# Six small moves in a one-layer hybrid decoder kernel: a third W buffer, later output products, a shorter head norm, a later z load, the norm row by DMA, a later turn for the gates

## The chip, the cores and the metric

The kernel runs on one core of a Trainium2 chip. The metric is the device time of one execution in microseconds (us), as the median of several runs. The engines are TensorE (PE in the profile; PEld is its weight load), VectorE (DVE), ScalarE (ACT), GpSimd (POOL) and SyncE (SP). SP and POOL are used here to issue DMAs. Each engine works through its own queue in a fixed order; between engines there are only semaphores.

## The reference

One layer of a decoder trunk for 1024 prompt rows and 8 single-token samples, all in float32, width 1024. The input is normalised by RMS and a gain row, goes through one combined projection (`w_in`, 1024 x 7176), and then through two branches. Cut to what matters here:

```python
hn = rmsnorm(x, g_norm)
xa, za, uq, uk, uv, uo, zb, ui, uf = split(hn @ w_in)
yA = rglru_branch(xa, ...)                     # gated linear recurrence
hB = mlstm_seq(uq, uk / 16, uv, ui + b_mi, log_sigmoid(uf + b_mf), ...)
# per chunk of 128 rows and head:
#   w = exp(D - m_t);  P = w * (q k^T)
#   num = P v + ginter * (q C);  den = sum(P) + ginter * (q n)
#   h = num / max(|den|, exp(-m_t));  C, n carried to the next chunk
yB = sigmoid(uo) * hB
yB = yB * rsqrt(mean(yB * yB) + EPS) * g_mhead # per head
merged = concat(yA * silu(za), yB * silu(zb))
y = rmsnorm(x + merged @ w_out, g_final)
```

The states of both branches are outputs too.

## The kernel before

**Precision.** Products run on float32r operands. Each operand is split in a high and a low half (`split`, L70 and L71: ScalarE writes the high half, VectorE the low one), and `mm3` (L64 to L66) makes three matmuls of each product.

**Order.** The source is written for a tile framework which gives every instruction its place in its engine's queue before the kernel runs. So the order of the source is not always the order of a queue, and each step is best followed in the profile's lines. A tile from a pool with `bufs=n` shares n buffers with the tiles of the same tag: a load into it waits until the tile n places earlier has been read for the last time.

**Start.** Nine row tiles of x (one of them the samples) are loaded by `x_fetch`; `x_stats` takes the sum of squares on ScalarE and the reciprocal root (L180, L184 to L188); `x_turn` multiplies by the root and by `gn_b`, the gain row broadcast to 128 partitions (L381), and transposes on TensorE (L385); `x_split` splits the transposed halves out of PSUM; `plain` makes the first products, with the weights `hi`, `lo` (first 256 columns and the 8 gate columns) and `w1` (the next 256). The broadcast row is made on TensorE from a loaded row `grow` and a matrix of ones (L488) and copied out of PSUM by VectorE (L490) and ScalarE (L492). Eight dummy matmuls (`warm_up`, L472) surround it.

**Projection.** Units of 512 columns (`UNITS`) are worked off with a scheme of seven products over half-size blocks (`cb`, `Q_P1` to `Q_P7`); `prep` makes and splits the weights of each, two products ahead. After every half of a product `pop_bg` takes the next steps from three lists: `bg` (two steps in the first and the last unit, else one), `rgq` (the recurrence) and `dcq` (the samples). `gates()` is a generator on `bg`: it loads parameters, makes the gate rows, two scans (L593, L594), the stacked rows `stk` (L612 to L615), yields eight times, transposes `stk` on TensorE (L622) and writes `be_t`, `gi_t`, `de_t`, `em_t`. `rd_open`, after it on the list, opens the pool for the recurrence and the samples and starts their loads.

**The mLSTM loop.** An item is a chunk of 128 rows and one head: n = 4c + h, 32 items. `m_load(n)` loads W (the row `d_alpha`, broadcast to 128 partitions, two buffers), qk and vt on SP's queue. `m_k(n)` makes the exponent of W (L1045 on VectorE, L1046 on ScalarE) and splits q and the state. `m_a(n)` makes S and the turned k on TensorE (L1065, L1067) into the PSUM tile `s`, of which there is one, and on VectorE `pf` (L1074, the last reader of W) and `kl` (L1075). `m_b(n)` makes the products with the state, k and v and updates the state (L1126). `m_g(n)` applies the output gate and takes the sum of squares per head. At h = 0 `m_n(c-1)` makes the norm of the chunk's four heads (L1151 to L1156, then `rsqrt`); at h = 1 `m_z(c-1, pair)` transposes the heads (L1173, into the PSUM tiles `s` and `qp`), multiplies by z (L1176) and splits.

**Output.** `out_part` makes the products with `w_out`, for a row tile c and a half of the columns; it's a generator on `work`, and `fill(k)` runs k of its pieces. Every item has four of them, placed between `m_a`, `m_k` and `m_b`. When a row tile is complete, L1272 adds x, and `finish` makes the norm and multiplies both halves by it and by the final gain (L1226) and stores them from POOL's queue (L1227). The next tile's x is loaded into the same staging buffers (L1271, POOL's queue). `last_tile` has an order of its own for the last row tile.

**Entry of the loop.** After the last unit `o_load(0)`, `m_k(4)`, `z_load(0)`, `wo_load` and `wo_prep` follow: z(0) is read from `d_zs`, which the last units have written; `wo_prep` (L1212, L1213) splits the last rows of `w_out`.

**Memory.** `const` tiles live for the whole kernel; `dconst` tiles lie in a pool that is closed at `m_open2`, where the loop's second pool takes its place.

Of the kernel before, what the change touches and what calls it, by code (L numbers as in the profile page):

```python
# [17 lines left out]
P = 128  # L18
# [31 lines left out]
def hymba_kernel(  # L50
# [17 lines left out]
    def split(hi, lo, src):  # L68

        A.copy(hi, src)  # L70
        V.tensor_tensor(lo, src, hi.bitcast(F32), op=ALU.subtract)  # L71
# [7 lines left out]
    def ps(tag, shape):  # L79
        return psp.tile(shape, F32, tag=tag, name=f"ps_{tag}", bufs=NBUF.get(tag, 1))  # L80

    def const(shape, name, dt=F32):
        return cpool.tile(shape, dt, tag=name, name=name)
# [10 lines left out]
    def ws(shape, name, dt=F32R):  # L94

        return wsp.tile(shape, dt, tag="ws", name=name)
# [12 lines left out]

    idF = const([P, P], "idF")  # L110
    make_identity(nc, idF)
    ones = const([P, P], "ones")
    G.memset(ones, 1.0)
    maskT = const([P, P], "maskT")
    G.memset(maskT, 0.0)
# [247 lines left out]
    def x_fetch(i):  # L363
        xt[i] = ws([P, T], f"x{i}", F32)
        ld(xt[i][:rows_of(i)], x_prompt[0, i * P:(i + 1) * P, :] if i < 8 else x_sample[:, 0, :])
# [20 lines left out]
            xps[i].append(pt)  # L386
        del xt[i]

    def x_split(i):

        p0, p1 = xps[i]
        if i == 8:
            for half, pt in enumerate(xps[i]):
                V.tensor_copy(hnd[:, 4 * half:4 * half + 4, 0:NB], pt[:, :, 0:NB])
            return
        s = slice(i % 4 * P, (i % 4 + 1) * P)
        if i >= 4:
            b12 = [fp.tile([P, 4, P], F32R, tag=f"b12{n}", name=f"b12{n}") for n in "hl"]
            split(b12[0], b12[1], p0)
            split(cb[Q_P3][0][:, :, s], cb[Q_P3][1][:, :, s], p1)  # L400
            bf[i] = b12
        else:
            split(cb[Q_P1][0][:, :, s], cb[Q_P1][1][:, :, s], p0)
            split(cb[Q_P2][0][:, :, s], cb[Q_P2][1][:, :, s], p1)

    def x_copy(i):

# [59 lines left out]

    pw = ps("tr", [P, P])

    def warm_up(n):  # L470
        for _ in range(n):
            TE.matmul(pw, ones, ones, start=True, stop=True)  # L472
    grow = ws([1, T], "grow", F32)
    ld(grow, g_norm)
    x_fetch(xorder[0])
    load_raw(0, 0, (0,))
    ld(wg, w_in[0, :, C_G:C_G + 8].rearrange("(k p) c -> p k c", p=P))
    load_raw(0, 1, (0,))
# [2 lines left out]
    load_raw(0, 1, (1,))  # L481
    ld(bgate[:, 0:4], b_mi[0].partition_broadcast(P))
    ld(bgate[:, 4:8], b_mf[0].partition_broadcast(P))
    warm_up(3)
    pg = []
    for half in range(2):
        pg.append(ps("o", [P, 512]))
        TE.matmul(pg[half], ones[0:1, :], grow[:, half * HT:(half + 1) * HT], start=True, stop=True)  # L488
    warm_up(5)
    V.tensor_copy(gn_b[:, 0:HT], pg[0])  # L490
    x_stats(xorder[0])
    A.copy(gn_b[:, HT:T], pg[1])  # L492
    x_stats(xorder[1])
    for m, i in enumerate(xorder):
        x_turn(m)
        if m == 0:
            split(hi[:, :, 256:264], lo[:, :, 256:264], wg)
            for b in range(2):
                for k in (4 * b, 4 * b + 2):
                    split(hi[:, k:k + 2, 0:256], lo[:, k:k + 2, 0:256], raws[0, b][:, k % 4:k % 4 + 2, 0:256])  # L500
                if b == 0:
                    x_split(i)
            for b in range(2):
                w1_split(b)
        else:
            x_split(i)
        if 4 <= i < 8:
            x_copy(i)
        if m + 2 < 9:
            x_fetch(xorder[m + 2])  # L510
            x_stats(xorder[m + 2])
        if i < 8:
            plain(i)
            x_combos(i)
# [16 lines left out]
    def gates():  # L531
# [81 lines left out]
        V.tensor_copy(stk[32:36], br)  # L613
        V.tensor_tensor(c3(stk[64:68]), c3(br), aL.unsqueeze(2).to_broadcast([NH, NCH, L]), op=ALU.add)
        V.tensor_scalar(stk[96:100], mr, -1.0, None, op0=ALU.mult)  # L615
        for _ in range(8):
            yield
        for half in range(2):
            pk = ps(("s", "qp")[half], [P, 4, P])
# [8 lines left out]
            yield  # L628
        ids = idF.rearrange("p (a g m) -> p a g m", a=2, g=2)
        V.tensor_tensor(sel, ids[:, 0], ids[:, 1], op=ALU.add)  # L630
        V.tensor_scalar(de_t, de_t, 1.0 / 16.0, None, op0=ALU.mult)

    bg, rgq, dcq = deque(), deque(), deque()
# [378 lines left out]
    def m_load(n):  # L1012
        if n >= 4 * NCH:
            return
        c, h = n // 4, n % 4
        ts_ = slice(c * L, (c + 1) * L)
        W = mx["p"].tile([P, L], F32, tag="W", name="W", bufs=2)
        ld(W, d_alpha[h:h + 1, ts_].rearrange("o t -> (o t)").partition_broadcast(P))
        qk = mx["p"].tile([P, 4, L], F32, tag="qk", name="qk", bufs=2)
        ld(qk, d_qk[h][:, :, ts_].rearrange("m p t -> p m t"))  # L1020
        vt = mx["p"].tile([P, 256], F32, tag="vt", name="vt", bufs=2)
        ld(vt, d_v[h][ts_, :])
        it[n] = {"qk": qk, "vt": vt, "W": W}

# [122 lines left out]
    def m_n(c):  # L1147

        m = ch[c]["m"]
        dn, ss, t, rs, u = (m[:, n] for n in range(5))  # L1150
        V.scalar_tensor_tensor(t, dn, -1.0, em_t[:, c, :], op0=ALU.mult, op1=ALU.max)  # L1151
        V.tensor_tensor(t, t, dn, op=ALU.max)
        V.tensor_scalar(t, t, (4 * 256 * EPS) ** 0.5, None, op0=ALU.mult)
        V.tensor_tensor(t, t, t, op=ALU.mult)
        V.tensor_tensor(t, t, ss, op=ALU.add)
        V.tensor_scalar(t, t, 1.0 / (4 * 256), 1e-37, op0=ALU.mult, op1=ALU.max)  # L1156
        rsqrt(rs, t, u)
        ch[c]["mh"], ch[c]["ml"] = ws([P, 8, P], f"mh{c}"), ws([P, 8, P], f"ml{c}")

# [56 lines left out]
    def fms():  # L1216
        return mx["p2"].tile([P, 4], F32, tag="fms", name="fms", bufs=2)

    def finish(n, yt, ms, dst):

        V.tensor_scalar(ms[:n, 0:1], ms[:n, 0:1], ms[:n, 1:2], 1.0 / T, op0=ALU.add, op1=ALU.mult)
        V.tensor_scalar(ms[:n, 0:1], ms[:n, 0:1], EPS, None, op0=ALU.add)
        rsqrt(ms[:n, 2:3], ms[:n, 0:1], ms[:n, 3:4])
        for half in range(2):
            hs = slice(half * HT, (half + 1) * HT)
            V.scalar_tensor_tensor(yt[half][:n], yt[half][:n], ms[:n, 2:3], mx["gf"][half][:n], op0=ALU.mult, op1=ALU.mult)  # L1226
            stq(dst[:, hs], yt[half][:n])  # L1227

    def dec_end():

# [23 lines left out]
    def out_part(c, half, part):  # L1254

        x = ot[c]
        if part == 0:
            x["p", half] = ps("o", [P, 512])
        mh, ml = x["r"] if part == 0 else (ch[c]["mh"], ch[c]["ml"])
        hs = slice(half * HT, (half + 1) * HT)  # L1260
        for k in range(8):
            w = wo[8 * part + k]
            mm3(x["p", half], mh[:, k, :], ml[:, k, :], w[:, 0, hs], w[:, 1, hs], part == 0 and k == 0, part == 1 and k == 7)
            if k % 2:
                yield
        if part == 1:
            if half == 0:
                x["ms"] = fms()
                x["y"] = [sg([P, HT], f"y{n}") for n in range(2)]
                for n in range(2):  # L1270
                    stq(x["y"][n], x_prompt[0, c * P:(c + 1) * P, n * HT:(n + 1) * HT])  # L1271
            V.tensor_tensor(x["y"][half], x["y"][half], x["p", half], op=ALU.add)  # L1272
            A.activation(x["p", half], x["y"][half], AF.Square, accum_out=x["ms"][:, half:half + 1])
            if half == 1:
                finish(P, x["y"], x["ms"], y_p[0, c * P:(c + 1) * P, :])
                del ot[c], ch[c]


# [67 lines left out]
            state["prep"] += 1  # L1346

    gg = gates()
    bg.extend([lambda: next(gg, None)] * 20 + [rd_open])
    last_u = len(units) - 1  # L1350
    unit_of = {p: u for u, pair in enumerate(units) for p in pair}
    done_h = [max(unit_of[k, h] for k in "qkv") for h in range(NH)]
# [48 lines left out]
                 out_part(1, 1, 0)])  # L1401
    o_load(0)
    m_k(4)
    z_load(0)
    wo_load(10)
    wo_prep(8)
    fill(2)
# [6 lines left out]
    for n in range(4, N):  # L1414
        c, h = n // 4, n % 4
        if h == 0 and c > 1:
            work.extend([out_part(c, 0, 0), out_part(c - 1, 0, 1), out_part(c - 1, 1, 1)])
            work.append(out_part(c, 1, 0) if c < last else last_part(0))
        m_a(n)
        so_load(n)  # L1420
        if n > 4:
            m_g(n - 1)
        m_load(n + 2)
        if h == 2:
            z_load(c)
        if h == 0:
            m_n(c - 1)
            fill(2)
            m_k(n + 1)
            fill(1)  # L1430
            if c == 1:
                wo_prep(12)
                wo_load(14)
                o_load(1)
            m_b(n)
            fill(1)
        elif h == 1:
            m_zg(c - 1)
            fill(1)
            m_k(n + 1)  # L1440
            fill(1)
            m_z(c - 1, 0)
            if c == 1:
                wo_prep(14)
            m_b(n)
            fill(1)
            m_z(c - 1, 1)
            fill(1)
            if c < last:
                o_load(c + 1)  # L1450
        else:
            fill(1)
            m_k(n + 1)
            fill(2)
            m_b(n)
            fill(1)
        if c == 1 and h > 0:
            next(dend, None)
# [7 lines left out]
    m_z(last, 1)  # L1466
    while work:
        fill(1)
    last_tile()
    es_m.close()  # L1470

# [32 lines left out]
```

## Time and profile before

| what | value |
|---|---|
| median of 3 runs | 987.69 us (986.12 to 987.83) |
| profiled execution, its own time | 994.51 us |
| its span, first to last instruction | 992.7 us |
| mean granted TensorE clock | 0.986 |
| HBM read, written | 100.07 MB, 51.65 MB |
| start and first row tiles, 0 to 80 us: TensorE busy | 25.64 + 49.33 us |
| projection, 80 to 690 us: TensorE busy | 482.57 + 118.23 us |
| last stretch, 975 to 992.7 us: TensorE busy | 11.16 us |

How to read it: a row of the profile's timeline is the start, the duration, the engine, the source line, the operation, output <- inputs, the shape, the count, and in brackets how long the engine had been idle before and what ended that. "SPq" and "POOLq" rows are the issue of a DMA, not its transfer. The waits view lists engine, line, what was waited for, then total, times and longest in us. "Granted clock" is the share of its full clock that TensorE was given.

### The profile page before, as it was taken

Reading aid. Unit: us, or ns where it says so; the run is one execution under the profiler, and the core shown is the slowest. Engines: PE = TensorE matmul, PEld = TensorE weight load, DVE = VectorE, ACT = ScalarE, POOL = GpSimd, SP = SyncE. Lnnn points to the kernel's source line nnn. Section 1 sums busy time; section 2 is a strip of 40 time slices with the busy share of each in tenths; the row PEclk is TensorE's granted clock in tenths of the full one; section 3 lists DMA queues with packets and bytes.
Section 4 is the critical chain, followed back from the end, with each engine's and each line's share of the span. In section 5 each row is a group of like instructions: output and inputs, shape, how many; then the busy total and the mean of one; then the engine's idle time right before and its main releaser. Section 6 shows DMA issues by size and latency. Waiting matters only on the chain. (4 is left out here: it accounts for less than half of the span.)

```text
span 992.7 us, 15370 instructions
## 1 busy us (share of the span) xinstructions
PE 952.1 (96%) x5396; PEld 775.2 (78%) x5396; DVE 702.3 (71%) x1463; ACT 543.1 (55%) x981; POOL 146.6 (15%) x259
## 2 busy tenths in 40 slices
PE   8999989999999999999999999999799998999997
PEld 7797767867788988777798997765568777878886
DVE  6785898887888778766876647676456566666664
ACT  6563446765666574635667544645445455546533
POOL 1111113021212122112213210100101000000020
PEclk9999999999999999999999999999999999999999
DMA  5431366366555647266536362337844454464341
GB/s 165 133 123 42 128 181 222 117 201 193 192 169 176 196 157 224 79 225 230 192 106 214 97 199 91 106 119 229 262 135 142 128 155 135 116 178 136 102 105 53
DMA packets 129173, 152.66 MB, mean 154 GB/s; under 512 B 13735, under 2 KB 107975, under 8 KB 129088
## 3 DMA queue, kind: packets, MB, share of 16 engines
q1 hardware_dynamic: 111368, 95.81, 32.7%
q0 software_dynamic: 17728, 55.87, 15.9%
q8 instruction: 42, 0.69, 0.3%
q14 instruction: 35, 0.29, 0.1%
HBM read 100.07 MB, written 51.65 MB: 153 GB/s over the span
## 5 line engine op out<-in xcount | busy, mean ns | idle before, releaser
L70 ACT CAST wh<-raw 128x1024 fp32r<-128x1024 f32 x91 | 95.4, 1050 | 72.2 <-PE ps_o L65 26.9
L71 DVE TENSOR_TENSOR wl<-raw,wh 128x1024 fp32r<-128x1024 f32 x91 | 110.9, 1219 | 33.3 <-ACT wh L70 23.3
L64 PE MATMUL ps_kv<-cb_hi,wh 128*128 128x512 f32 x320 | 128.1, 400 | 0.0
L66 PE MATMUL ps_kv<-cb_hi,wl 128*128 128x512 f32 x320 | 125.5, 392 | 0.0
L65 PE MATMUL ps_kv<-cb_lo,wh 128*128 128x512 f32 x320 | 125.3, 391 | 0.0
L64 PE MATMUL ps_o<-cb_hi,wh 128*128 128x512 f32 x240 | 95.5, 398 | 0.1
L66 PE MATMUL ps_o<-cb_hi,wl 128*128 128x512 f32 x240 | 94.4, 393 | 0.0
L65 PE MATMUL ps_o<-cb_lo,wh 128*128 128x512 f32 x240 | 94.3, 393 | 0.0
L64 PEld LDWEIGHTS ps_kv<-cb_hi,wh 128*128 128x128 f32 x320 | 60.1, 188 | 24.6 <-issue 6.8
L66 PEld LDWEIGHTS ps_kv<-cb_hi,wl 128*128 128x128 f32 x320 | 60.1, 188 | 15.3 <-issue 2.5
L65 PEld LDWEIGHTS ps_kv<-cb_lo,wh 128*128 128x128 f32 x320 | 60.2, 188 | 11.7
L1045 DVE SCALAR_TENSOR_TENSOR W<-W,be_t,maskT 128x128 f32<-128x128 f32 x32 | 11.2, 352 | 78.0 <-DMA W<-d_alpha 78.0
L64 PE MATMUL ps_o<-wo,rh 128*128 128x512 f32 (+1 forms) x136 | 54.1, 398 | 1.4 <-DMA rh<-d_rm 1.4
L64 PE MATMUL ps_kv<-wh,cb_hi 128*128 128x256 f32 x192 | 55.3, 288 | 0.0
L65 PE MATMUL ps_kv<-wl,cb_hi 128*128 128x256 f32 x192 | 54.3, 283 | 0.0
L66 PE MATMUL ps_kv<-wh,cb_lo 128*128 128x256 f32 x192 | 54.3, 283 | 0.0
L64 PEld LDWEIGHTS ps_o<-cb_hi,wh 128*128 128x128 f32 x240 | 45.4, 189 | 11.3 <-issue 1.7
L66 PEld LDWEIGHTS ps_o<-cb_hi,wl 128*128 128x128 f32 x240 | 45.5, 190 | 10.4 <-issue 0.8
L64 PE MATMUL ps_o<-wo,mh 128*128 128x512 f32 (+1 forms) x136 | 53.4, 393 | 0.0
L65 PEld LDWEIGHTS ps_o<-cb_lo,wh 128*128 128x128 f32 x240 | 45.6, 190 | 9.1
L66 PE MATMUL ps_o<-wo,ml 128*128 128x512 f32 (+1 forms) x136 | 52.4, 386 | 0.0
L66 PE MATMUL ps_o<-wo,rl 128*128 128x512 f32 (+1 forms) x136 | 52.3, 384 | 0.1
(472 smaller groups left out, 2569.7 us busy)
## 6 DMA issues: line engine op xcount, KB each, us to landing
raw<-in_w_in_dram SPq DMA_DIRECT2D x56, 512.0 KB
Cb<-in_state_mlstm_C_dram SPq DMA_DIRECT2D x32, 256.0 KB
out_dram<-Cb POOLq DMA_DIRECT2D x32, 256.0 KB, 4.3
qk<-d_qk SPq DMA_DIRECT2D x32, 256.0 KB
oraw<-in_w_out_dram SPq DMA_DIRECT2D x16, 512.0 KB
d_qk<-s POOLq DMA_DIRECT2D x24, 256.0 KB, 4.1
x<-in_x_prompt_dram SPq DMA_DIRECT2D x8, 512.0 KB
d_x<-s POOLq DMA_DIRECT2D x16, 256.0 KB, 2.9
```

Of the source, the lines that this page charges most:

```text
L64: TE.matmul(out, ah, bh, start=first, stop=False, skip_group_check=True)
L65: TE.matmul(out, ah, bl, start=False, stop=False, skip_group_check=True)
L66: TE.matmul(out, al, bh, start=False, stop=last, skip_group_check=True)
L70: A.copy(hi, src)
L71: V.tensor_tensor(lo, src, hi.bitcast(F32), op=ALU.subtract)
L1045: V.scalar_tensor_tensor(W, W, be_t[:, c, h:h + 1], maskT, op0=ALU.add, op1=ALU.min)
```

## The change

It does seven things:

- `W` has three buffers; to make room, `ones` moves from the lasting pool to the pool that is closed at `m_open2`.
- `finish` for the prompt's row tiles 0 to 6 puts the two last multiplications and stores on a list, `tails`, which `tail()` empties at the items with h = 2 and 3, and once before `last_tile`.
- The head norm has two operations fewer per chunk: the factor goes into one combined operation, and the lower bound is put once on `em_t`.
- `z_load(0)` moves from ahead of the weights at the loop's entry to item 4, after `m_load(6)`.
- The gain row is loaded broadcast to 128 partitions by one DMA (512 KB) behind the first x tile and ahead of the weights; the row tile, its matmuls and copies go; 17 dummy matmuls stand in the place of 8.
- `x_split` is divided by halves, and for the first tile the weights' splits are interleaved with it.
- `gates()` yields 14 times instead of 8 before the transposes, and 26 turns instead of 20 stand on the list ahead of `rd_open`.

```diff
-    ones = const([P, P], "ones")
+    ones = dconst([P, P], "ones")
...
-    def warm_up(n):
-        for _ in range(n):
-            TE.matmul(pw, ones, ones, start=True, stop=True)
-    grow = ws([1, T], "grow", F32)
-    ld(grow, g_norm)
+    for _ in range(17):
+        TE.matmul(pw, ones, ones, start=True, stop=True)
     x_fetch(xorder[0])
+    ld(gn_b, g_norm[0].partition_broadcast(P))
     load_raw(0, 0, (0,))
...
-    warm_up(3)
-    pg = []
-    for half in range(2):
-        pg.append(ps("o", [P, 512]))
-        TE.matmul(pg[half], ones[0:1, :], grow[:, half * HT:(half + 1) * HT], start=True, stop=True)
-    warm_up(5)
-    V.tensor_copy(gn_b[:, 0:HT], pg[0])
     x_stats(xorder[0])
-    A.copy(gn_b[:, HT:T], pg[1])
     x_stats(xorder[1])
     for m, i in enumerate(xorder):
         x_turn(m)
         if m == 0:
+            def w0_split(k):
+                split(hi[:, k:k + 2, 0:256], lo[:, k:k + 2, 0:256], raws[0, k // 4][:, k % 4:k % 4 + 2, 0:256])
+            w0_split(0)
             split(hi[:, :, 256:264], lo[:, :, 256:264], wg)
-            for b in range(2):
-                for k in (4 * b, 4 * b + 2):
-                    split(hi[:, k:k + 2, 0:256], lo[:, k:k + 2, 0:256], raws[0, b][:, k % 4:k % 4 + 2, 0:256])
-                if b == 0:
-                    x_split(i)
+            x_split(i, 0)
+            w0_split(2)
+            x_split(i, 1)
+            w0_split(4)
+            w0_split(6)
...
-        for _ in range(8):
+        for _ in range(14):
             yield
...
+        V.tensor_scalar(em_t, em_t, 1e-15, None, op0=ALU.max)
...
-        W = mx["p"].tile([P, L], F32, tag="W", name="W", bufs=2)
+        W = mx["p"].tile([P, L], F32, tag="W", name="W", bufs=3)
...
-        V.tensor_scalar(t, t, (4 * 256 * EPS) ** 0.5, None, op0=ALU.mult)
-        V.tensor_tensor(t, t, t, op=ALU.mult)
-        V.tensor_tensor(t, t, ss, op=ALU.add)
-        V.tensor_scalar(t, t, 1.0 / (4 * 256), 1e-37, op0=ALU.mult, op1=ALU.max)
+        V.scalar_tensor_tensor(t, t, EPS, t, op0=ALU.mult, op1=ALU.mult)
+        V.scalar_tensor_tensor(t, ss, 1.0 / (4 * 256), t, op0=ALU.mult, op1=ALU.add)
...
+    tails = []
+
+    def tail():
+        while tails:
+            tails.pop(0)()
+
-    def finish(n, yt, ms, dst):
+    def finish(n, yt, ms, dst, later=False):
...
-        for half in range(2):
-            hs = slice(half * HT, (half + 1) * HT)
-            V.scalar_tensor_tensor(yt[half][:n], yt[half][:n], ms[:n, 2:3], mx["gf"][half][:n], op0=ALU.mult, op1=ALU.mult)
-            stq(dst[:, hs], yt[half][:n])
+
+        def out():
+            for half in range(2):
+                hs = slice(half * HT, (half + 1) * HT)
+                V.scalar_tensor_tensor(yt[half][:n], yt[half][:n], ms[:n, 2:3], mx["gf"][half][:n], op0=ALU.mult, op1=ALU.mult)
+                stq(dst[:, hs], yt[half][:n])
+        if later:
+            tails.append(out)
+        else:
+            out()
...
-                finish(P, x["y"], x["ms"], y_p[0, c * P:(c + 1) * P, :])
+                finish(P, x["y"], x["ms"], y_p[0, c * P:(c + 1) * P, :], True)
...
-    bg.extend([lambda: next(gg, None)] * 20 + [rd_open])
+    bg.extend([lambda: next(gg, None)] * 26 + [rd_open])
...
     m_k(4)
-    z_load(0)
     wo_load(10)
...
         m_load(n + 2)
-        if h == 2:
-            z_load(c)
+        if h == 2 or n == 4:
+            z_load(c if h == 2 else 0)
...
         else:
             fill(1)
+            tail()
             m_k(n + 1)
...
     while work:
         fill(1)
+    tail()
     last_tile()
```

More of the change, by code (lines that the diff above doesn't have):

```diff
@@ L387, in x_turn, with x_split @@
         del xt[i]
-    def x_split(i):
-        p0, p1 = xps[i]
+    def x_split(i, half):
+        p = xps[i][half]
         if i == 8:
-            for half, pt in enumerate(xps[i]):
-                V.tensor_copy(hnd[:, 4 * half:4 * half + 4, 0:NB], pt[:, :, 0:NB])
+            V.tensor_copy(hnd[:, 4 * half:4 * half + 4, 0:NB], p[:, :, 0:NB])
             return
         s = slice(i % 4 * P, (i % 4 + 1) * P)
[L397 to L401, printed above, removed]
-        else:
-            split(cb[Q_P1][0][:, :, s], cb[Q_P1][1][:, :, s], p0)
-            split(cb[Q_P2][0][:, :, s], cb[Q_P2][1][:, :, s], p1)
+        if i >= 4 and half == 0:
+            bf[i] = [fp.tile([P, 4, P], F32R, tag=f"b12{n}", name=f"b12{n}") for n in "hl"]
+            split(*bf[i], p)
+        else:
+            q = Q_P3 if i >= 4 else (Q_P1, Q_P2)[half]
+            split(cb[q][0][:, :, s], cb[q][1][:, :, s], p)
     def x_copy(i):
@@ L505, in hymba_kernel @@
         else:
-            x_split(i)
+            x_split(i, 0)
+            x_split(i, 1)
         if 4 <= i < 8:
```

## The prediction

> **What bounds the kernel now.** I read the page first, then a table by stage, then the waits of TensorE, then of all engines, then timelines. The page's first lines:
>
> ```profile
> span 992.7 us, 15370 instructions
> PE 952.1 (96%) x5396; PEld 775.2 (78%) x5396; DVE 702.3 (71%) x1463; ACT 543.1 (55%) x981; POOL 146.6 (15%) x259
> ```
>
> TensorE is busy for 952.1 of 992.7 us, so no edit that leaves its matmuls alone can take away more than its 40.6 idle us, plus what a reduced clock costs. The diff leaves every product of the layer as it is, so I look for the idle. Busy time by stage (columns: stretch; its length; PE, PEld, DVE, ACT, POOL busy; granted clock; DMA share; GB/s):
>
> ```profile
> 690.00:730.00 40.00, 32.79 (x157) 21.78 (x156) 19.10 (x31) 17.77 (x29) 4.34 (x8) 0.91 0.73 232
> 730.00:975.00 245.00, 232.42 (x1294) 198.35 (x1294) 155.56 (x491) 125.83 (x334) 22.03 (x38) 0.98 0.48 133
> ```
>
> 7.2 us are idle in the 40 us before the mLSTM loop settles and 12.6 us in the loop's 245 us. TensorE's own waits name the causes (total, times, longest):
>
> ```profile
> PE ps_s L1173 <- DVE ms L1141: 10.7, 5, 2.7
> PE ps_qp L64 <- ACT hh L1121: 6.0, 2, 5.8
> ```
>
> Five chunk boundaries cost 10.7 us, one wait at the loop's entry 5.8 us. Among all engines one wait stands out:
>
> ```profile
> DVE W L1045 <- DMA W<-d_alpha: 78.0, 31, 5.8
> ```
>
> VectorE stands 78.0 us at L1045. Mostly TensorE has other work meanwhile: it lacks work only in the places above.
>
> **The change part by part.** All times are of the profiled execution: 994.51 us by its own clock, its span 992.7, so 1.8 us lie outside. The median of the runs shown is 987.69; I sum against 994.51 and scale by 987.69/994.51 = 0.9931.
>
> *Norm row by DMA.* At the start the statistics wait behind the copies of the broadcast row:
>
> ```profile
> 5.72 0.18 ACT L370 ACTIVATION_READ_ACCUMULATOR junk<-x 128x1 f32 x1
> 7.14 0.14 DVE L180 TENSOR_SCALAR st<-st 128x1 f32<-128x1 f32 x1
> 10.23 1.41 DVE L381 SCALAR_TENSOR_TENSOR x<-x,st,gn_b 128x512 f32<-128x512 f32 x2
> 11.08 1.94 PE L385 MATMUL ps_kv<-idF,x 128*128 128x128 f32 x8 [2.16 <-issue]
> 14.72 0.15 DVE L180 TENSOR_SCALAR st<-st 128x1 f32<-128x1 f32 x1 [0.36 <-ACT junk L370]
> 15.97 0.16 DVE L188 SCALAR_TENSOR_TENSOR st<-st 128x1 f32<-128x1 f32 x1
> 20.54 0.39 PE L65 MATMUL ps_o<-w1l,cb_hi 128*128 128x256 f32 x1 [0.21 <-DVE w1l L71]
> ```
>
> The sum of squares is read by 5.90, yet L180 starts at 7.14, behind the copy of the row, and L381 at 10.23. The second tile's chain, undisturbed, takes 16.13 - 14.72 = 1.41 us from L180 to the end of L188. So L381 could start at 5.90 + 0.2 + 1.4 = 7.5, 2.7 us earlier. TensorE's first real wait afterwards, at 20.54, is for VectorE's split of the weights, so VectorE's lead carries through; the 17 dummy matmuls lie in time in which TensorE has nothing else. Against it stands a 512 KB transfer ahead of the weights:
>
> ```profile
> 4.00:8.00 4.00, 4.00 (x7) 1.35 (x5) 0.75 (x2) 1.15 (x2) 0.00 (x0) 1.00 1.12 341
> gf<-in_g_final_dram POOLq DMA_DIRECT2D x2, 256.0 KB, 7.6
> ```
>
> At the 341 GB/s moved there, 512 KB are 1.5 us; a broadcast of this kind, two halves from POOL amid other traffic, took 7.6. At 1.5 it lands by about 6.3 (x was in by 4.75), before 7.5; at 7.6 at about 12, and the gain turns into a loss of some 2. The nearest row is the 341 GB/s of this place, on this queue. I take 2.5 us gained; bounds -2.7 and +2.
>
> *Three buffers for W.* By the code, item n+1's exponent (m_k) stands between m_a(n) and m_b(n). What the engines did (VectorE, then SyncE's queue):
>
> ```profile
> 575.57 0.35 DVE L1045 SCALAR_TENSOR_TENSOR W<-W,be_t,maskT 128x128 f32<-128x128 f32 x1 [1.61 <-DMA W<-d_alpha]
> 577.95 0.35 DVE L1045 SCALAR_TENSOR_TENSOR W<-W,be_t,maskT 128x128 f32<-128x128 f32 x1 [0.38 <-DMA W<-d_alpha]
> 580.75 0.28 DVE L1074 SCALAR_TENSOR_TENSOR pf<-ps_s,W 128x128 f32<-128x128 f32 x1
> 586.01 0.35 DVE L1045 SCALAR_TENSOR_TENSOR W<-W,be_t,maskT 128x128 f32<-128x128 f32 x1 [3.06 <-DMA W<-d_alpha]
> 590.82 0.29 DVE L1074 SCALAR_TENSOR_TENSOR pf<-ps_s,W 128x128 f32<-128x128 f32 x1 [1.09 <-ACT kh L1073]
> ```
> ```profile
> 581.06 0.32 SPq L1018 DMA_DIRECT2D W<-d_alpha  x1
> ```
>
> The third L1045 runs before the second L1074: item 2's exponent stands ahead of item 1's product. The order isn't the code's: an instruction is put where its operands were expected ready. W(2) is loaded the moment L1074 of item 0 frees the buffer (580.75, DMA at 581.06), and L1045 is queued for its landing, so VectorE waits out the transfer although nobody needs W(2) for another item. With three buffers L1074 of item n frees the buffer of W(n+3), and by the same rule L1045(n+3) is queued for that landing: the same wait at the same place, one item further ahead. I take 0. Bounds: 0, and all that VectorE's wait costs TensorE (second rival). The cover is that TensorE has four groups of out-products per item.
>
> *Products two items later, shorter norm.* A boundary, VectorE and ScalarE first, TensorE last:
>
> ```profile
> 864.57 1.28 ACT L184 ACT_TABLE_LOAD   x1
> 865.18 0.17 DVE L1156 TENSOR_SCALAR ms<-ms 128x4 f32<-128x4 f32 x1
> 867.00 0.35 DVE L1045 SCALAR_TENSOR_TENSOR W<-W,be_t,maskT 128x128 f32<-128x128 f32 x1 [1.65 <-DMA W<-d_alpha]
> 868.13 1.42 DVE L1226 SCALAR_TENSOR_TENSOR y<-y,fms,gf 128x512 f32<-128x512 f32 x2
> 869.46 0.48 DVE L1126 SCALAR_TENSOR_TENSOR Cf<-Cf,cs_b,ps_kv 128x258 f32<-128x258 f32 x1
> 872.68 0.63 PE L1173 MATMUL ps_s<-idF,hh 128*128 128x128 f32 x4 [2.39 <-DVE ms L1141]
> ```
>
> VectorE runs back to back from 867.00 until L1173 may start. The two products of the row before take 869.46 - 868.13 = 1.33 us of it. Put behind, they take 1.33 from each of the five waits: 6.65 of 10.7, and 4.0 stay. Bounds: 6.65, and 0 if L1126 was not expected ready there, so that the products stay in front. I take 6.65, since L1126 follows without a pause. The norm loses two operations of 0.17 per chunk, but its square root can't start before the table load ends at 864.57 + 1.28 = 865.85, and L1156 has ended at 865.35; so 0, at most 0.35 for each of 8 chunks (2.8). The added maximum on em_t is one operation of that size, once.
>
> *Gates' turn later.* The transposes of the gate rows, on TensorE:
>
> ```profile
> 127.14 0.39 PE L65 MATMUL ps_kv<-cb_lo,wh 128*128 128x512 f32 x1
> 129.56 0.63 PE L622 MATMUL ps_s<-idF,stk 128*128 128x128 f32 x4 [2.03 <-DVE stk L614]
> 130.38 0.48 PE L66 MATMUL ps_kv<-cb_hi,wl 128*128 128x512 f32 x1
> ```
>
> L622 stands inside a triple of the next unit's product, not where the code yields: again the place of expected readiness. Six more yields need not move it. I take 0; bounds -2.0 (the wait goes) and +2 (the recurrence's loads, opened six turns later, come late).
>
> *z's first load later.* The loop's entry, SyncE, VectorE, ScalarE:
>
> ```profile
> 706.27 0.38 SPq L1037 DMA_DIRECT2D z<-d_zs  x1
> 712.41 0.35 DVE L1045 SCALAR_TENSOR_TENSOR W<-W,be_t,maskT 128x128 f32<-128x128 f32 x1 [4.21 <-DMA W<-d_alpha]
> 714.72 1.15 ACT L1212 ACTIVATE wo<-oraw,gm 128x1024 fp32r<-128x1024 f32 x1 [1.62 <-DMA oraw<-in_w_out_dram]
> ```
>
> z waits for its stores at the head of SyncE's queue; W and the last weights issue behind it, and ScalarE's L1121, for which TensorE waits 5.8 us, comes behind L1212. In the new code z still precedes those weights' load, and W(7) is queued as W(6) was. I take 0; bound -9.1, from the 5.8 and the clock below.
>
> *Clock.* Two stretches:
>
> ```profile
> 870.00:878.00 8.00, 5.61 (x29) 4.99 (x28) 5.46 (x16) 4.49 (x13) 1.47 (x3) 0.79 0.87 238
> 712.00:724.00 12.00, 6.88 (x19) 4.23 (x20) 6.51 (x14) 5.37 (x11) 0.00 (x0) 0.72 0.75 227
> ```
>
> (1 - 0.79) x 8 = 1.7 us are lost after a wait of 2.39 us, (1 - 0.72) x 12 = 3.4 after 5.8. Since about 1 us of wait stays at boundaries, I take no gain; bound -3.4 for two boundaries. The Trainium skill ("TensorE: Matmul & The Clock Gate", Part 1) has the clock halved after an idle window of about 3.4 us; the stretch at 870 disagrees, with 2.39. By the page closing a boundary would never return clock; by the row it may.
>
> **Sum**: -2.5 - 6.65 = -9.15, so 994.51 - 9.15 = 985.4, times 0.9931: **978.6 us**.
>
> **The rivals.** *Only the start pays*: queues filled by expected readiness keep the products, W and z where they were, so these edits don't do what they say. -2.5: 992.0, 985.2 us. For it: L1045 and L622 are placed that way; against it: L1126 right behind L1226.
>
> *VectorE's wait for W goes*: if L1045 stays where the code has it, the third buffer gives the transfer an item's time. Then the other 4.0 us at the boundaries go, and the entry's 5.8 + 3.4: 985.4 - 13.2 = 972.2, or 965.5 us, and 3.4 less with the boundaries' clock, 962. For it: the wait is 78.0 us; against it: L1045 already runs an item ahead.
>
> *Late products hold the row's buffers* (slower). The chain and POOL:
>
> ```profile
> 873.05 0.54 POOL L1271 DMA_DIRECT2D y<-in_x_prompt_dram  x1 [0.68 <-DMA out_dram<-y]
> 890.27 0.59 DVE y L1272
> ```
>
> The next row's y is loaded only when the last row's store has left the buffer: 873.05 is 4.9 us after the products' start, and the transfer follows: W's took under 5 us (581.06 to 586.01), I take 3 as an estimate. If the products really run two items (16 us) later, near 886, y lands near 894, 3.7 us after L1272 needs it at 890.27. VectorE then stands before L1074 and L1075, for which TensorE has, by these two rows, 848.26 - 847.36 = 0.9 us to spare:
>
> ```profile
> 846.89 0.47 DVE L1075 SCALAR_TENSOR_TENSOR kl<-ps_s,de_t,kh 128x256 fp32r<-128x256 f32 x1
> 848.26 0.28 PE L64 MATMUL ps_kv<-vh,kh 128*128 128x258 f32 x1
> ```
>
> 2.8 us for each of six rows is 16.8: 985.4 + 16.8 = 1002.2, 995.3 us. It decides from a product start of about 883; up to there y lands in time.
>
> **How the numbers follow.** Forecast 0.40, W's wait goes 0.20, only the start 0.18, late products 0.13, and 0.09 that the start is given back (the row's transfer) with nothing else. A measurement tells about 0.2%, 2 us, from no change. Faster: 0.40 + 0.20 + most of 0.18 = 0.75; same 0.12; slower 0.13. The range leaves out the last rival and the lower end of the second: 962 to 989.
>
> **What would show it.** Right: L381 starts near 7.5; L1045's wait stays near 78 us, with the fourth L1045 ahead of the second L1074; L1226 stands behind L1075 and the waits of L1173 fall to about 4 us; L622 and the wait at 711 stay. Wrong: L1045's wait gone and the entry closed (second rival), L1226 still before L1126 (first), L1272 waiting for y (third), or L381 waiting for gn_b.

## The result and the profile after

| | before | after |
|---|---|---|
| median of 4 runs each | 987.76 us (986.12 to 988.63) | 974.08 us (971.12 to 975.99) |
| profiled execution, its span | 992.7 us | 973.3 us |
| mean granted TensorE clock | 0.986 | 0.993 |

The ratio is 0.986, with a 95% interval from 0.983 to 0.989: 1.4% faster, near the forecast of 978.6 us. The experiments show that the forecast had about the right size for wrong reasons. Lines have other numbers in the changed kernel: L1037 was L1045, L1067 was L1075, L1113 was L1121, L1163 was L1173, L1224 was L1226.

The page's first lines and its busy times by stage (stretch, length, busy PE, PEld, DVE, ACT, POOL, granted clock, DMA share, GB/s), after:

```profile
PE 943.5 (97%) x5410; PEld 770.3 (79%) x5410; DVE 699.9 (72%) x1447; ACT 542.8 (56%) x980; POOL 147.1 (15%) x259
```
```profile
690.00:730.00 40.00, 35.80 (x183) 24.37 (x182) 22.33 (x40) 19.47 (x34) 4.35 (x8) 1.00 0.79 259
730.00:960.00 230.00, 226.84 (x1290) 193.92 (x1289) 151.74 (x470) 124.55 (x329) 22.11 (x38) 1.00 0.53 138
```

In the loop 3.2 of 230 us are idle instead of 12.6 of 245, at the entry 4.2 instead of 7.2, and the granted clock is 1.00 in both stretches (0.98 and 0.91 before). TensorE's waits and VectorE's wait for W, after (total, times, longest):

```profile
PE ps_o L66 <- DVE ml L71: 2.5, 3, 1.3
...
PE ps_s L613 <- DVE stk L605: 2.2, 1, 2.2
PE ps_qp L64 <- ACT hh L1113: 1.6, 1, 1.6
...
PE ps_s L1163 <- DVE ms L1133: 0.5, 1, 0.5
```
```profile
DVE W L1037 <- DMA W<-d_alpha: 48.4, 26, 4.4
```

The boundary waits fell from 10.7 to 0.5 us, not to the forecast 4.0, and VectorE's wait for W from 78.0 to 48.4 us, where no change was forecast. The gates' wait stayed (2.0, now 2.2).

**Where the time came from.** The transposes into `ps_s` at h = 1 mark the chunks. Their first and sixth, before and after:

```profile
762.70 0.60 PE L1173 MATMUL ps_s<-idF,hh 128*128 128x128 f32 x4
...
944.75 0.90 PE L1173 MATMUL ps_s<-idF,hh 128*128 128x128 f32 x4 [2.59 <-DVE ms L1141]
```
```profile
758.13 0.60 PE L1163 MATMUL ps_s<-idF,hh 128*128 128x128 f32 x4
...
926.75 0.60 PE L1163 MATMUL ps_s<-idF,hh 128*128 128x128 f32 x4
```

Up to the first mark the change gains 4.6 us, over the five chunks between the marks 182.05 - 168.62 = 13.4, and from the last mark to the end of the span 47.95 - 46.55 = 1.4. That is the 19.4 us between the two spans. The profiled execution before was a long one, 994.51 us beside a median of 987.76, so the change itself is worth 13.7 of them. The first mark lies between 753.9 and 762.7 us in all the traces of this document, whatever the edit, so the 4.6 us are no sign of anything. The chunks are where the change pays: a chunk takes 33.7 us instead of 36.4, and in all five traces with two buffers and W's transfer the five chunks take 179.0 to 183.4 us, in all eight with three buffers 165.2 to 170.7.

**The start.** TensorE and VectorE, after:

```profile
6.81 1.41 DVE L381 SCALAR_TENSOR_TENSOR x<-x,st,gn_b 128x512 f32<-128x512 f32 x2
...
9.90 0.39 PE L64 MATMUL ps_o<-wph,b12h 128*128 128x264 f32 x1 [0.96 <-ACT b12h L70]
...
15.77 0.38 PE L65 MATMUL ps_o<-w1l,b12h 128*128 128x256 f32 x1 [0.92 <-DVE w1l L71]
...
22.08 0.39 PE L64 MATMUL ps_o<-wph,cb_hi 128*128 128x264 f32 x1 [0.90 <-ACT cb_hi L70]
```

L381 starts 3.4 us earlier than before (10.23) and waits for no row. But then TensorE waits for the splits of the weights and of x, again and again: 3.9 us in five waits up to 29 us, against 0.2 before. The product with the samples' rows (L509) starts at 29.12 us, against 28.93 before: the lead of 3 us is spent by then.

**W's order.** VectorE, after:

```profile
581.11 0.28 DVE L1066 SCALAR_TENSOR_TENSOR pf<-ps_s,W 128x128 f32<-128x128 f32 x1
...
586.85 0.35 DVE L1037 SCALAR_TENSOR_TENSOR W<-W,be_t,maskT 128x128 f32<-128x128 f32 x1 [1.62 <-DMA W<-d_alpha]
...
591.66 0.29 DVE L1066 SCALAR_TENSOR_TENSOR pf<-ps_s,W 128x128 f32<-128x128 f32 x1 [1.09 <-ACT kh L1065]
```

586.85 is the fourth exponent, and it stands ahead of the second product, as forecast. The order was right; that it makes the third buffer worthless was not.

**A boundary**, after:

```profile
855.04 0.35 DVE L1037 SCALAR_TENSOR_TENSOR W<-W,be_t,maskT 128x128 f32<-128x128 f32 x1 [0.62 <-DMA W<-d_alpha]
...
856.16 0.75 DVE L1224 SCALAR_TENSOR_TENSOR y<-y,fms,gf 128x512 f32<-128x512 f32 x1
856.83 0.87 DVE L1118 SCALAR_TENSOR_TENSOR Cf<-Cf,cs_b,ps_kv 128x258 f32<-128x258 f32 x2
...
857.95 0.75 DVE L1224 SCALAR_TENSOR_TENSOR y<-y,fms,gf 128x512 f32<-128x512 f32 x1
```

The output products haven't left the boundary: one stands ahead of the state update L1118, the other right behind it, and both ahead of the transposes at 860.71. Yet TensorE doesn't wait there. So something else closed the boundary.

### The profile page after: what moved, and what is told of

Its sections match the earlier page's. It is cut to its first block, busy times and chain, and to the rows that moved or that the text cites. A ratio compares the mean times of both kernels' runs of the same rounds, so it can differ in the third digit from the quotient of the medians.

```text
span 973.3 us, 15380 instructions
## 1 busy us (share of the span) xinstructions
PE 943.5 (97%) x5410; PEld 770.3 (79%) x5410; DVE 699.9 (72%) x1447; ACT 542.8 (56%) x980; POOL 147.1 (15%) x259
## 4 chain that ended last, share of the span: by engine, by line
PE 49%; DMA 5%; DVE 3%; ACT 1%; issue 1%; SPq 0%; ACTq 0%; DVEq 0%
PE ps_o L66 9%; PE ps_o L64 8%; PE ps_o L65 8%; PE ps_kv L64 5%; PE ps_kv L66 5%; PE ps_kv L65 4%; DMA W<-d_alpha 2%; DMA rh<-d_rm 1%; PE ps_s L1057 1%; PE ps_tr L1193 1%; PE ps_tr L227 1%; DMA rl<-d_rm 1%; PE ps_qp L64 1%; DMA raw<-in_w_in_dram 1%; PE ps_qp L66 1%
## 5 line engine op out<-in xcount | busy, mean ns | idle before, releaser
L64 PE MATMUL ps_o<-wo,rh 128*128 128x512 f32 (+1 forms) x136 | 53.5, 394 | 1.3 <-DMA rh<-d_rm 1.2
L65 PE MATMUL ps_o<-wo,rh 128*128 128x512 f32 (+1 forms) x136 | 51.8, 381 | 0.0
```

Of the source, the lines that this page charges most:

```text
L64: TE.matmul(out, ah, bh, start=first, stop=False, skip_group_check=True)
L65: TE.matmul(out, ah, bl, start=False, stop=False, skip_group_check=True)
```

## Experiments

The times are medians; each ratio is against runs of the kernel before on the same chip. Those runs scatter from 984 to 997 us, so 2 or 3 us between two kernels tell little.

### The change without its third buffer

```diff
-        W = mx["p"].tile([P, L], F32, tag="W", name="W", bufs=3)
+        W = mx["p"].tile([P, L], F32, tag="W", name="W", bufs=2)
```

> The changed kernel (974.1 us) with two buffers for W again. Theory A (the third buffer only moves VectorE's wait one item further, as its queue shows: in the changed kernel the fourth L1037 at 586.85 us stands ahead of the second L1066 at 591.66): 974 us, within 2; the waits at the boundaries and at the loop's entry stay as in the changed kernel. Theory B (the third buffer lets W land earlier, and that is what closed the boundaries and the entry; VectorE's wait for W fell from 78.0 to 48.4 us): some 984 us or more, W's wait near 78 us again, boundary waits of TensorE back towards 10 us.

Measured: 994.37 us, ratio 1.007 (1.004 to 1.010). The waits of L1163 for `ms` are back at 9.7 us, VectorE's wait for W at 74.7. Theory A, which is the forecast's, falls: without the third buffer the rest of the change is slower than the kernel before. `ones` lies in its new place here too, so making room isn't what pays. The waits of TensorE and VectorE in this run:

```profile
PE ps_s L1163 <- DVE ms L1133: 9.7, 5, 2.5
```
```profile
DVE W L1037 <- DMA W<-d_alpha: 74.7, 29, 9.9
```

### The third buffer alone

```diff
-    ones = const([P, P], "ones")
+    ones = dconst([P, P], "ones")
...
-        W = mx["p"].tile([P, L], F32, tag="W", name="W", bufs=2)
+        W = mx["p"].tile([P, L], F32, tag="W", name="W", bufs=3)
```

> The kernel before with W's third buffer alone (and the room made for it). Theory B (the third buffer is the whole gain; with two buffers the rest of the change made 994 us): 971 to 974 us, boundary waits of TensorE under 4 us, W's wait near 48 us. Theory C (the buffer gains only together with the late products): at least 980 us, and some boundary waits of 2 us left.

Measured: 972.67 us, ratio 0.981 (0.977 to 0.985). The one edit gives the whole gain. TensorE from 870 to 940 us, before and then with the third buffer alone:

```profile
870.00:940.00 70.00, 65.98 (x370) 57.26 (x369) 43.83 (x140) 35.93 (x97) 3.65 (x7) 0.98 0.50 143
```
```profile
870.00:940.00 70.00, 70.00 (x407) 61.17 (x406) 48.00 (x150) 39.48 (x104) 7.75 (x13) 1.00 0.54 134
```

Busy for 70.00 of 70.00 us: in this stretch the loop is bound by TensorE. Its marks show the chunk:

```profile
760.12 0.60 PE L1173 MATMUL ps_s<-idF,hh 128*128 128x128 f32 x4
...
925.27 0.60 PE L1173 MATMUL ps_s<-idF,hh 128*128 128x128 f32 x4
```

165.15 us for five chunks, 33.0 each; the kernel before took 36.4.

**What the buffer does.** One chunk of the kernel before on VectorE, from one `kl` (L1075, which follows the last use of W directly) to the fourth after it, with the next load on SyncE's queue:

```profile
800.25 0.47 DVE L1075 SCALAR_TENSOR_TENSOR kl<-ps_s,de_t,kh 128x256 fp32r<-128x256 f32 x1
...
805.15 0.35 DVE L1045 SCALAR_TENSOR_TENSOR W<-W,be_t,maskT 128x128 f32<-128x128 f32 x1 [2.92 <-DMA W<-d_alpha]
...
810.63 0.48 DVE L1075 SCALAR_TENSOR_TENSOR kl<-ps_s,de_t,kh 128x256 fp32r<-128x256 f32 x1
...
814.88 0.35 DVE L1045 SCALAR_TENSOR_TENSOR W<-W,be_t,maskT 128x128 f32<-128x128 f32 x1 [3.51 <-DMA W<-d_alpha]
...
819.51 0.47 DVE L1075 SCALAR_TENSOR_TENSOR kl<-ps_s,de_t,kh 128x256 fp32r<-128x256 f32 x1
...
836.48 0.47 DVE L1075 SCALAR_TENSOR_TENSOR kl<-ps_s,de_t,kh 128x256 fp32r<-128x256 f32 x1
```
```profile
800.58 0.38 SPq L1018 DMA_DIRECT2D W<-d_alpha  x1
```

The chain closes on itself: the last use of W frees the buffer, the load is issued (800.58), VectorE stands until it lands (805.15), does the rest of the item up to the next last use (just ahead of 810.63), and only then is the next load issued. VectorE and the transfer form a ring. Four turns of it are one chunk, 836.48 - 800.25 = 36.2 us, whichever engine sets the pace; what fills them tells which one does (columns as in the table by stage):

```profile
800.25:836.48 36.23, 33.39 (x188) 28.50 (x188) 22.93 (x73) 18.85 (x50) 1.92 (x4) 1.00 0.50 138
```

VectorE works for 22.9 us of the four turns, waits 10.9 for W and 2.2 for other engines; TensorE is busy for 33.4 only. TensorE has work in hand for most of each turn, so the shortfall shows once per chunk, at the boundary. The same chunk with the third buffer alone, taken one turn later:

```profile
803.02 0.48 DVE L1075 SCALAR_TENSOR_TENSOR kl<-ps_s,de_t,kh 128x256 fp32r<-128x256 f32 x1
...
808.55 0.48 DVE L1075 SCALAR_TENSOR_TENSOR kl<-ps_s,de_t,kh 128x256 fp32r<-128x256 f32 x1
808.94 0.34 DVE L1045 SCALAR_TENSOR_TENSOR W<-W,be_t,maskT 128x128 f32<-128x128 f32 x1
...
812.32 0.35 DVE L1045 SCALAR_TENSOR_TENSOR W<-W,be_t,maskT 128x128 f32<-128x128 f32 x1 [2.56 <-DMA W<-d_alpha]
...
836.33 0.47 DVE L1075 SCALAR_TENSOR_TENSOR kl<-ps_s,de_t,kh 128x256 fp32r<-128x256 f32 x1
```

Three of the four turns still contain a landing. The first, from 803.02 to 808.55, has none and takes 5.5 us; the same turn of the kernel before is its second, from 810.63 to 819.51, which took 8.9 with a wait of 3.51 for W. The exponent of the W whose load was issued at the start of this turn follows at 808.94 without a wait: by then it had landed. One landing fewer per chunk brings the four turns to 33.3 us, about what TensorE needs. Over the five chunks between the marks, VectorE's waits for W went from 20 to 15, before and then with the third buffer alone:

```profile
DVE W L1045 <- DMA W<-d_alpha: 54.9, 20, 5.8
```
```profile
DVE W L1045 <- DMA W<-d_alpha: 34.8, 15, 3.0
```

### The kernel before without W's transfer

```diff
-        ld(W, d_alpha[h:h + 1, ts_].rearrange("o t -> (o t)").partition_broadcast(P))
...
-        V.scalar_tensor_tensor(W, W, be_t[:, c, h:h + 1], maskT, op0=ALU.add, op1=ALU.min)
+        V.scalar_tensor_tensor(W, maskT, be_t[:, c, h:h + 1], maskT, op0=ALU.add, op1=ALU.min)
```

> The kernel before, two buffers, with W's transfer left out: the exponent is made from the mask alone, same instruction, same place, so the decay weights and with them the output are other numbers. Theory D (VectorE and W's transfer form a ring: the last use of W frees the buffer, the load is issued, VectorE stands for it, and its work up to the next last use follows; a chunk of this ring is 36.2 us, TensorE's own work in a chunk 33.1): with the transfer gone the ring is under 30 us, TensorE is the bound, 968 to 974 us, no boundary wait over 1 us. Theory E (the third buffer helps by the order it gives and not by the transfer): 985 to 989 us.

Measured: 967.06 us, ratio 0.978 (0.974 to 0.981). With two buffers and no transfer the gain is there too, perhaps a few us more than the third buffer gives (the intervals overlap); no boundary waits, and a chunk takes 32.8 us. It is the landing in the ring that cost, not the number of buffers as such. Theory E falls. This run also takes 32 loads off SyncE's queue and the DMA engines; but the third buffer gains nearly as much and leaves them all there.

### The late products

Alone on the kernel before (the edit is the change's `finish`, `tails` and `tail()`):

> The kernel before with the late products alone. The forecast's step: 6.65 us off the waits of L1173, 981 us. By the run with two W buffers (994.4 us): no gain, and if the late products are what costs its 7 us, 990 to 994 us with W's wait longer at its longest (9.9 us there).

Measured: 997.28 us, ratio 1.007 (1.005 to 1.010), slower. VectorE and TensorE at a boundary, and the waits:

```profile
864.04 0.35 DVE L1045 SCALAR_TENSOR_TENSOR W<-W,be_t,maskT 128x128 f32<-128x128 f32 x1 [1.59 <-DMA W<-d_alpha]
...
865.18 0.75 DVE L1234 SCALAR_TENSOR_TENSOR y<-y,fms,gf 128x512 f32<-128x512 f32 x1
...
868.64 0.75 DVE L1234 SCALAR_TENSOR_TENSOR y<-y,fms,gf 128x512 f32<-128x512 f32 x1
869.30 0.28 DVE L1074 SCALAR_TENSOR_TENSOR pf<-ps_s,W 128x128 f32<-128x128 f32 x1
...
870.12 0.63 PE L1173 MATMUL ps_s<-idF,hh 128*128 128x128 f32 x4 [2.19 <-DVE kl L1075]
```
```profile
PE ps_s L1173 <- DVE kl L1075: 10.0, 5, 2.8
```

The products were placed between the same exponent and the same last use of W, so the turn of the ring is as long as before, and L1173 waits 10.0 us, now behind `kl` instead of `ms`. That is why the step gains nothing. In these two traces the loss lies at the last boundary. W's load and the exponent that waits for it there, with the late products and then in the kernel before:

```profile
942.24 0.38 SPq L1018 DMA_DIRECT2D W<-d_alpha  x1
```
```profile
952.86 0.35 DVE L1045 SCALAR_TENSOR_TENSOR W<-W,be_t,maskT 128x128 f32<-128x128 f32 x1 [8.86 <-DMA W<-d_alpha]
```
```profile
944.46 0.39 SPq L1018 DMA_DIRECT2D W<-d_alpha  x1
```
```profile
948.17 0.35 DVE L1045 SCALAR_TENSOR_TENSOR W<-W,be_t,maskT 128x128 f32<-128x128 f32 x1 [1.79 <-DMA W<-d_alpha]
```

10.6 us from issue to use instead of 3.7: 6.9 us, in a place where the ring hands them on. The stretch from the last boundary to the end is 6.7 us longer in that trace. Whether the late products make it land late isn't shown: it took 8.5 us also in the trace of the new start alone, which leaves the products at their old place and has the median of the kernel before. Why this transfer lands late stays open (last section).

The changed kernel with the products at their old place, and the kernel before with the third buffer and the late products:

```diff
-                finish(P, x["y"], x["ms"], y_p[0, c * P:(c + 1) * P, :], True)
+                finish(P, x["y"], x["ms"], y_p[0, c * P:(c + 1) * P, :])
```

> The changed kernel with the last rows' products where the source had them before (at the row's end). Theory A (the products were what stood ahead of the state update at a boundary): the boundary waits return, 6.7 us and with the clock up to 15: 981 to 988 us. Theory B (W's third buffer closed the boundaries): 974 us, within 2. In the changed kernel one product still stands ahead of the state update at 856.16 us and the other right behind it, so a middle value, 977 to 980, would say that only the second product moved.

Measured: 971.59 us, ratio 0.983 (0.980 to 0.987).

> The kernel before with W's third buffer and the late products. If the late products add nothing once W is early: within 2 us of the run with the third buffer alone. If they cost when the next row's load waits for them: 2 to 3 us more than that run, as the changed kernel is 2.5 us above its version with the products at their old place. If they gain: 2 us or more below it.

Measured: 975.16 us, ratio 0.984 (0.980 to 0.987). Both times the version with late products is 2.5 us above its partner, within the scatter: with the third buffer they gain nothing, and may cost a little.

### The products left out

```diff
-            V.scalar_tensor_tensor(yt[half][:n], yt[half][:n], ms[:n, 2:3], mx["gf"][half][:n], op0=ALU.mult, op1=ALU.mult)
+            if n < P:
+                V.scalar_tensor_tensor(yt[half][:n], yt[half][:n], ms[:n, 2:3], mx["gf"][half][:n], op0=ALU.mult, op1=ALU.mult)
```

> The kernel before with the two last products left out for the prompt's row tiles 0 to 6 (y is stored without its norm and gain). Theory D (work in the ring counts wherever it stands; moved it gains nothing, removed it gains its length): 1.33 us for each of five to seven boundaries, so 978 to 981 us, the boundary waits 1.3 us shorter each. If VectorE's work at the boundary doesn't matter at all: 987 us, waits as before.

Measured: 994.25 us, ratio 1.005 (1.003 to 1.008). A miss: the 1.33 us per boundary didn't come off the time. Between its marks (760.69 and 939.73) the five chunks take 179.04 us, 3.0 less than before, 0.6 per chunk. In these chunks VectorE works 7.3 us less (107.99 for 115.26), but waits 2.2 us more for W (57.1 for 54.9) and 2.1 more for the other engines; TensorE's waits at the five boundaries are 8.6 us, now behind ScalarE's `ph`, where 1.33 us less for each would have left 4.0. And at the last boundary W came late here too, 10.0 us after its issue (939.21 to 949.16). So in this trace work taken out of the ring was worth less than half its length, and the time of the whole hung on one late transfer. Why the other waits took up the rest wasn't tried: the sum of the ring's parts doesn't foretell what each part is worth.

### The start

```diff
-    for _ in range(17):
-        TE.matmul(pw, ones, ones, start=True, stop=True)
-    x_fetch(xorder[0])
-    ld(gn_b, g_norm[0].partition_broadcast(P))
+    grow = ws([1, T], "grow", F32)
+    ld(grow, g_norm)
+    x_fetch(xorder[0])
...
+    warm_up(3)
+    pg = []
+    for half in range(2):
+        pg.append(ps("o", [P, 512]))
+        TE.matmul(pg[half], ones[0:1, :], grow[:, half * HT:(half + 1) * HT], start=True, stop=True)
+    warm_up(5)
+    V.tensor_copy(gn_b[:, 0:HT], pg[0])
```

The old start (with the old `x_split`) in the changed kernel:

> The changed kernel with the start of the kernel before (row through TensorE, eight dummy matmuls, old order of the splits). Theory A (the 3 us that the first transposes gain are lost again by 29 us, since the weights land later; at 695 us the changed kernel is 0.4 us behind): 974 us or up to 1 us less. Theory B (the gain of the start survives, as forecast, 2.5 us): 976.6 us.

Measured: 971.52 us, ratio 0.984 (0.981 to 0.986). And the new start alone in the kernel before:

> The kernel before with the new start alone. Forecast's step: 2.5 us off, 984.8 us. By the run with the old start (2.6 us less than the changed kernel) and the traces (0.4 us behind at 695 us): 988 to 990 us, the first plain product waiting for ScalarE's and VectorE's splits of the weights.

Measured: 989.79 us, ratio 1.000 (0.997 to 1.004). The forecast's 2.5 us are in neither. Whether the new start costs a little (2.6 us by the first run, 0.6 by the second) the scatter doesn't tell.

### z, the norm and the gates

```diff
     m_k(4)
+    z_load(0)
     wo_load(10)
...
-        if h == 2 or n == 4:
-            z_load(c if h == 2 else 0)
+        if h == 2:
+            z_load(c)
```

> The changed kernel with the first load of z back ahead of the weights at the loop's entry. If z at the head of SyncE's queue made the entry's wait (TensorE 5.8 us before, 1.6 us after, and the half clock behind it, 3.4 us): 974.1 + 4.2 + 3.4 = 982 us, and the granted clock from 712 to 724 near 0.72 again. If the entry closed through W's third buffer: 974 us, within 2, and no half clock there.

Measured: 974.0 us, ratio 0.986 (0.983 to 0.989), the changed kernel's time. SyncE's queue shows why. The changed kernel, with the later call, and then the last weights in the kernel before:

```profile
706.38 0.38 SPq L1029 DMA_DIRECT2D z<-d_zs  x1
706.93 0.98 SPq L1179 DMA_DIRECT2D oraw<-in_w_out_dram  x2
```
```profile
707.92 0.85 SPq L1189 DMA_DIRECT2D oraw<-in_w_out_dram  x2
```

z still stands ahead of the last weights, at 706.38 us as against 706.27 before: the source moved the call, but not the load. Only W and qk, which were issued between the two, no longer are. The entry's wait for `hh` differs among the traces: 1.1 to 3.4 us in the six with the later call (1.6 after), 3.2 to 5.9 in the eight without it (5.8 before, 4.1 in this run, 3.5 with the third buffer alone). So the later call may shorten this wait; no time here shows a gain from it.

```diff
-        for _ in range(14):
+        for _ in range(8):
             yield
...
-        V.scalar_tensor_tensor(t, t, EPS, t, op0=ALU.mult, op1=ALU.mult)
-        V.scalar_tensor_tensor(t, ss, 1.0 / (4 * 256), t, op0=ALU.mult, op1=ALU.add)
+        V.tensor_scalar(t, t, (4 * 256 * EPS) ** 0.5, None, op0=ALU.mult)
+        V.tensor_tensor(t, t, t, op=ALU.mult)
+        V.tensor_tensor(t, t, ss, op=ALU.add)
+        V.tensor_scalar(t, t, 1.0 / (4 * 256), 1e-37, op0=ALU.mult, op1=ALU.max)
```

> The changed kernel with the old head norm and the old turn of the gates. Forecast 0 for both: 974 us, within 2. If the shorter norm gains its 0.35 us in each of 8 chunks: 977 us. If the gates' turn counts: up to 2 us either way, with another wait at the transposes than the 2.2 us of the changed kernel.

Measured: 973.74 us, ratio 0.985 (0.981 to 0.988): no difference beyond the scatter, and the gates' wait is 2.3 us as against 2.2.

### Old start and old place of the products together

> The changed kernel with the old start and the products at their old place: third buffer, short norm, later z, later gates. If the 2.6 and 2.5 us by which each of the two runs stood below the changed kernel are real and add up: 969 us. If they are scatter: 971 to 974 us, as the third buffer alone gave 972.7.

Measured: 970.72 us, ratio 0.982 (0.979 to 0.985). It lies between the two values expected, and its interval overlaps those of the changed kernel and of the third buffer alone. The two 2.5 us aren't shown to add up, and no version here is shown to beat the third buffer alone.

## Why the prediction came out near

The time was 4.5 us below the forecast and inside the range, and the sign was right; but the sum's two paying terms were not what paid. That the total came near is luck: a term taken at 0 brought more than the two together were to bring. By its own signs the forecast was wrong: L1045's wait fell by 29.6 us, the waits of L1173 went to 0.5 us and not to 4, the products stayed at the boundary, and the entry's wait fell.

- **Three buffers for W, taken at 0: the step that failed.** It is worth 16.6 us (989.23 to 972.67), all of the gain. The forecast reasoned that "VectorE waits out the transfer although nobody needs W(2) for another item", and that a third buffer gives "the same wait at the same place, one item further ahead". The order held at the place that it names (586.85), but in one item of four the exponent came after the landing, and its wait went: 15 waits are left of 20. The deeper error was to judge the wait by its place in one item and not to close the chain: the wait delays the next last use, and this delays the next load. Such a wait isn't covered by VectorE being an item ahead. The profile before could have told: in the four turns of one chunk (36.2 us) VectorE waited 10.9 us for W and 2.2 for anything else, while TensorE was busy for 33.4.
- **Output products, -6.65: failed.** The products moved within the ring, and the waits of L1173 stayed at 10.0 us with this edit alone. Reading "VectorE runs back to back from 867.00" as the whole cause left out that 867.00 itself was the end of a wait for W.
- **Norm row, -2.5: failed** at "VectorE's lead carries through". L381 did start even earlier than forecast (6.81), but the next limit was the splits of the weights and of x, and the 3 us were gone by 29 us.
- **Shorter norm, gates, z at 0: right, within the scatter.** The gates' wait stayed, and z's load kept its place at 706.38, both as forecast. The entry's wait, which was to stay, was 1.6 us in the trace; which edit shortened it isn't settled.
- **Clock, 0: mis-sized.** The loop's clock rose from 0.98 to 1.00 and the entry's from 0.91 to 1.00, while the waits went. With the third buffer alone TensorE's busy time in the five chunks fell from 169.85 to 165.00 us for the same 941 matmuls: 4.9 of the 16.9 us by which the chunks got shorter. The other 12 are idle time.
- **The rivals.** "VectorE's wait for W goes" came nearest to the mechanism, and named the wait of 78.0 us as its evidence; its price was too high, since 48.4 us of the wait stay. "Late products hold the row's buffers" had the right sign for that edit alone, but not the cause: VectorE shows no wait for y in that trace. "Only the start pays" was right that the products and z hardly moved, but the start didn't pay and W's buffer did. That the start is given back came true, though not "with nothing else".

## What to carry to other kernels

Where an in-order engine waits for a load whose buffer it frees itself, follow the chain from the last use through the load to the next last use; if it closes, add up over one period what is work in it and what is waiting for the load, and see whether the busiest engine is idle for part of that period, before asking who waits at the end of it. Here moving work to another place of the ring gained nothing; taking one landing per period out of it, with one more buffer of 64 KB, did. And where a framework places instructions by expected readiness, look in the queue whether an edit of the source's order moved anything: here the z load and the output products hardly moved.

## What the runs showed of the hardware

One transfer of 64 KB had very different times at the same place. At the last boundary W needed 3.7 us from issue to use in the kernel before, but 12.0 us in the change without the third buffer, 10.6 with the late products alone, 8.5 with the new start alone and 10.0 without the products. Stores of y and of the state and the next loads run at that time; which of them holds it up wasn't tried. The order of issue alone doesn't decide it: before and with the new start alone the state's store is issued 0.82 us ahead of W, and W took 3.7 and 8.5 us. With three buffers the last W is issued an item earlier (916.15 us with the third buffer alone, 9.1 ahead of the last mark), and the stretch behind that mark is 46.5 or 46.6 us in all eight traces, against 48.0 to 57.0 in the five with two buffers and the transfer. So in these traces the third buffer also keeps the end of the kernel out of reach of this scatter.

After a single idle of 2.84 us TensorE's clock fell in the run with the late products alone (in the second row the granted clock is the third value from the end):

```profile
942.65 0.63 PE L1173 MATMUL ps_s<-idF,hh 128*128 128x128 f32 x4 [2.84 <-DVE kl L1075]
```

```profile
944.00:946.00 2.00, 2.00 (x11) 2.00 (x11) 0.01 (x1) 1.56 (x4) 0.00 (x0) 0.50 1.16 84
```

The Trainium skill ("TensorE: Matmul & The Clock Gate", Part 1) names an idle window of about 3.4 us for this; the row shows half the clock after a shorter one.
